# Crossbar-transposed halves joined behind the next chunk's taking apart, and kept in the slots of the later splits

## The chip, the cores and the metric

One core of one Trainium2 chip runs the whole program. The metric is the device time of one execution in microseconds; before the change it is 1086.96 us (median of 3 runs, 1085.1 to 1087.68).

## The reference, cut to what matters

Two layers; in each a half-step SwiGLU FFN, an attention mix of two branches, and a second half-step FFN. The tokens are 256, the width 1024, the FFN's inner width 2816. All is float32.

```python
def swiglu(x, w_gate, w_up, w_down):
    return (jax.nn.silu(x @ w_gate) * (x @ w_up)) @ w_down

for l in range(DEPTH):
    x = x + 0.5 * swiglu(rms_norm(x, ffn1_norm[l]), ffn1_w_gate[l], ffn1_w_up[l], ffn1_w_down[l])
    h = rms_norm(x, mix_norm[l])
    ...
    x = x + merged @ w_out[l]
    x = x + 0.5 * swiglu(rms_norm(x, ffn2_norm[l]), ffn2_w_gate[l], ffn2_w_up[l], ffn2_w_down[l])
```

## The kernel before, in words

**Products in three parts.** Every float32 operand is split into a high part (a copy rounded to the matmul's type) and a low part (the rest), and a product is three matmuls: high by high, high by low, low by high (`three`, lines 169 to 172). `split_to` (185) makes the two parts: ScalarE writes the high one (line 186, tiles wh, hi, corner, uh, vh), VectorE subtracts for the low one (187, tiles wl, lo, ul, vl). The weights stream from HBM in tiles of 512 KB: SyncE's queue (SP) loads them into a ring of four raw slots (142 and 353), and `parts` (133) splits them into a ring of six.

**The FFN** (`ffn`, 314) is called four times, two in each layer. The inner width is cut into 11 chunks of 256. For each chunk, *gate-up* runs one projection of 24 matmuls (`project`, 277) for each of the two token tiles t = 0, 1 into a PSUM bank "g", of which there are two. `glu` (447) empties it: ScalarE applies Silu to the gate half (452), VectorE multiplies by the up half (453), and both write the tile hh of the chunk. So the projection after next waits for this hh's VectorE step.

The down product needs hh transposed as float32 values are, while its layout comes from a crossbar DMA that transposes 16-bit elements. So `send` (321) takes hh apart into 16-bit halves on ScalarE (323, tile z16, "z" in the views), and SP issues the crossbar transpose into zT (325). `arrive` (328), called one chunk later than the following send, joins the halves again on ScalarE (335, tile a), adds and subtracts blocks on VectorE (340, four instructions) and splits the result into hi and lo (186, 187), which stay until the down product. `PLAN` (52) says for each chunk whether it goes into the down product plainly ("S", chunks 0, 9 and 10: four blocks, no additions) or by seven products instead of eight ("F" and "G": seven blocks). For the seven, sums of weight blocks are needed as well: `differences` (356) computes u and v from two raw rows on VectorE (357), and for three of the chunks `prepare` does so ahead, in the gate-up stage (`PREP`, 53 and 54); the others do it in `sevens` (380) during the down product. `combine` (420) folds the seven banks together at the end (p, line 427).

Who goes first. TensorE's order is as written in the code. The order on ScalarE, VectorE and SP is set by a scheduler at build time, which may move an instruction past others unless a dependency forbids it. Two rules stand in the code: `issue_after(last_hi[0])` puts the join behind the last high part written so far, and `arrive` is called at the start of chunk c for the half sent at the end of chunk c − 2. In the down product `arrive` is called in the first part and once from the third chunk on (383). Each engine works through its queue in order, so what waits holds up all behind it.

z16 shares a pair of buffers ("xg") with hh and others; zT has one buffer, and u, v and a share two ("sums").

Of the kernel before, what the change touches and what calls it, by code (L numbers as in the profile page):

```python
# [11 lines left out]
F32 = mybir.dt.float32  # L12
F32R = mybir.dt.float32r
I32 = mybir.dt.int32
BF16 = mybir.dt.bfloat16
U16 = mybir.dt.uint16
AF = mybir.ActivationFunctionType
# [5 lines left out]
P = 128  # L23
D = 1024
S = 256
# [3 lines left out]
KD = D // P  # L29
FC = 256  # L30
NFC = FF // FC
# [20 lines left out]
PLAN = "SFGFGGFGGSS"  # L52
PREP = {3: 1, 5: 3, 7: 6}
PREP_FIRST = {5: 1, 7: 3, 8: 6}
NS = sum(kind != "S" for kind in PLAN)
# [3 lines left out]
def hybrid_encoder(ctx, tc, x, w_gu1, w_d1, w_in, b_gate, qk_gain, rpb, sink, t5,  # L59
                   w_bna, w_bsw, w_out, w_gu2, w_d2, c_mask, c_band, out):  # L60
    nc = tc.nc
# [3 lines left out]
    act = ctx.enter_context(tc.tile_pool(name="act", bufs=1))  # L65
# [58 lines left out]
    def linked(engine, emit):  # L124
        with ExitStack() as order:
            if engine in chain:
                order.enter_context(tc.issue_after(chain[engine].ins))
            inst = emit()
        if chain:
            chain[engine] = inst  # L130
        return inst

    def parts(r, nk=2, n=512):
        wh = ring.tile([P, 2, 512], F32R, name="wh", tag="wh", bufs=RING)
        wl = ring.tile([P, 2, 512], F32R, name="wl", tag="wl", bufs=RING)
        split_to(wh[:, :nk, :n], wl[:, :nk, :n], r)
        return wh, wl

    def load(src, nk, n):
        raw = ring.tile([P, 2, 512], F32, name="raw", tag="raw", bufs=RAW)  # L140
        r = raw[:, :nk, :n]
        nc.sync.dma_start(r, src)
        return parts(r, nk, n)

    def columns(w, l, c0, n, nk=KD):
        return [load(w[l, 2 * i * P:(2 * i + 2) * P, c0:c0 + n].rearrange("(k p) n -> p k n", p=P), 2, n)
                for i in range(nk // 2)]

    def rows(w, l, k):
        return load(w[l, k * P:(k + 1) * P, :].rearrange("p (h n) -> p h n", h=2), 2, 512)  # L150
# [4 lines left out]
    def defer(lag, key, fn):  # L155
        later.append((now[0] + lag, len(later), key, fn))
        later.sort(key=lambda e: e[0])
# [25 lines left out]
    last_hi = [None]  # L183

    def split_to(hi, lo, src):
        last_hi[0] = linked("act", lambda: nc.scalar.activation(hi, src, AF.Copy))  # L186
        linked("dve", lambda: nc.vector.tensor_tensor(lo, src, hi.bitcast(F32), ALU.subtract))  # L187
# [126 lines left out]
    def ffn(l, n, w_gu, w_d, after):  # L314
        with tc.tile_pool(name="ffn", bufs=1) as fp:
            hs = {}
            SLOT = ((1, 2), (0, 3))

            on_way = []

            def send(c, hh):
                z = act.tile([P, 2, 4 * P], U16, name="z16", tag="xg", bufs=2)
                nc.scalar.activation(z, hh.bitcast(U16).rearrange("p s (n two) -> p two (s n)", two=2), AF.Copy)  # L323
                zT = fp.tile([P, 2 * 4, P], U16, name="zT", tag="zT")
                nc.sync.dma_start_transpose(zT, z.rearrange("p two n -> p (two n)"))
                on_way.append((c, zT))

            def arrive():
                c, zT = on_way.pop(0)
                m = 4 if PLAN[c] == "S" else 7  # L330
                hi = fp.tile([P, m, P], F32R, name=f"hi{m}", tag=f"hi{m}", bufs=NS if m == 7 else NFC - NS)
                lo = fp.tile([P, m, P], F32R, name=f"lo{m}", tag=f"lo{m}", bufs=NS if m == 7 else NFC - NS)
                a = fp.tile([P, 8, P], F32, name="a", tag="sums", bufs=2)
                with tc.issue_after(last_hi[0].ins):
                    nc.scalar.activation(a[:, :4, :].bitcast(U16).rearrange("p s (n two) -> p two (s n)", two=2),  # L335
                                         zT.rearrange("p (two s) n -> p two (s n)", two=2), AF.Copy)
                if m == 7:
                    for to, x, y, op in ((4, 0, 3, ALU.add), (6, 1, 0, ALU.subtract), (5, 4, 1, ALU.subtract),
                                         (7, 2, 5, ALU.subtract)):
                        nc.vector.tensor_tensor(a[:, to, :], a[:, x, :], a[:, y, :], op)  # L340
                    split_to(hi, lo, a[:, 1:, :])
                else:
                    split_to(hi, lo, a[:, :4, :])
                hs[c] = (hi, lo)

            def get(t, k):
# [4 lines left out]
            def block_row(k, c0=0, n=2):  # L351
                r = ring.tile([P, 2, 512], F32, name="raw", tag="raw", bufs=RAW)[:, :n, :]
                nc.sync.dma_start(r, w_d[l, k * P:(k + 1) * P, :n * 512].rearrange("p (h n) -> p h n", h=n))
                return r
# [19 lines left out]
            def sevens(c):  # L374
                r0 = block_row(2 * c, n=1 if c in stored else 2)
                r1 = block_row(2 * c + 1)
                place = ("xh0", "xl0", "xh1", "xl1")[(c - PLAN[:c].count("S")) % 4]
                both = act.tile([P, 2, 512], F32R, name="corner", tag=place)
                corner = [both[:, i, :] for i in range(2)]
                split_to(*corner, r0[:, 0, :])  # L380
                low = parts(r1)
                us, vs = stored.get(c) or differences(r0, r1, lambda name, r: parts(r))
                if on_way and c >= 2:
                    arrive()
                half = lambda pair, i: [p[:, i, :] for p in pair]
                return (("1", 0, corner), ("2", 1, half(low, 0)), ("3", 6, half(low, 1)), ("5", 3, half(us, 1)),
                        ("6", 4, half(vs, 0)), ("4", 2, half(vs, 1)), ("7", 5, half(us, 0)))
# [67 lines left out]
            for c in range(NFC):  # L455
# [4 lines left out]
                elif n == 0 and c == 1:  # L460
                    pieces = second
                else:
                    pieces = columns(w_gu, l, c * 512, 512)
# [29 lines left out]
    def mix(l, n, after):  # L493
        with tc.tile_pool(name="mix", bufs=1) as mp:
# [223 lines left out]
            def gated(br, acc, t, d):  # L718
                g = gate[br][:, t, d, :]
                nc.vector.scalar_tensor_tensor(g, g, 1.0, acc, op0=ALU.add, op1=ALU.mult)  # L720

            def local(d):
                pieces = columns(w_bsw, l, d * 512, 512, 4)
                for t in range(T):
                    acc = ps_g.tile([P, 512], F32, name="g", tag="g")
                    branch(1, acc, t, pieces, range(4))
                    gated(1, acc, t, d)
# [7 lines left out]
                split_to(*(m[:, 4 * d:4 * d + 4, :] for m in mT[t]), tp)  # L735

            def grid(d):
                pieces = columns(w_bna, l, d * 512, 512, 4)
                acc = [ps_acc.tile([P, 512], F32, name="br", tag="sc", bufs=2) for _ in range(T)]
                for ks in ((0, 1, 2), (3,)):  # L740
                    for t in range(T):
                        branch(0, acc[t], t, pieces, ks)
                for t in range(T):
                    gated(0, acc[t], t, d)
                    g = gate[0][:, t, d, :]
                    nc.vector.tensor_tensor(g, g, gate[1][:, t, d, :], ALU.add)
                    defer(M_LAG, ("merge", t, d), lambda t=t: merge(t, d))

            for d in range(2):
                local(d)  # L750
                grid(d)
# [99 lines left out]
```

## Time and profile before

| | us |
|---|---|
| median of 3 runs | 1086.96 |
| the profiled execution | 1086.75 |
| its span | 1085.0 |
| TensorE busy (PE) | 1059.2 |
| VectorE busy (DVE) | 878.1 |
| ScalarE busy (ACT) | 747.8 |

Times in the views are counted from the span's start. In the rows, L186 is line 186 of the kernel before; "out<-in" are tiles without their numbers; what stands in square brackets is the idle time before an instruction and what ended it. A matmul's recorded length is longer than the distance to the next one, because matmuls are pipelined. The first layer's FFN 1 takes about the first 190 us, its FFN 2 about 366 to 545; the second layer's FFNs stand at about 549 to 727 and 902 to 1085.

### The profile page before, as it was taken

What the parts mean: (1) busy time and instruction counts of PE and PEld (TensorE: products, weight loads), DVE (VectorE), ACT (ScalarE), POOL (GpSimd) and SP (SyncE); (2) the same over time, 40 slices, a digit from 0 to 9 for tenths busy, and PEclk for the clock granted to TensorE, in tenths of its full rate; (3) what the DMA queues carried; (4) which work ended last, traced back from release to release, by engine and by line L of the source; (5) the groups of instructions that cost most, each with busy time, mean ns of one, the idle gap of its engine ahead of it and who ended that gap; (6) DMA issues with size and microseconds to landing.
All of it is one profiled execution on the core that took longest, in us unless ns stands there. A gap on an engine that the chain in (4) does not pass through costs nothing.

```text
span 1085.0 us, 14545 instructions
## 1 busy us (share of the span) xinstructions
PE 1059.2 (98%) x4949; PEld 871.0 (80%) x4949; DVE 878.1 (81%) x1337; ACT 747.8 (69%) x1070; POOL 117.2 (11%) x118
## 2 busy tenths in 40 slices
PE   9999899999999999999999999999999999999998
PEld 7887787888888888778788778778888888877886
DVE  6677889889886868878977886998898866788796
ACT  6776855788773667776567777657887646778662
POOL 1000040244420000000000000003524100000000
PEclk9999999999999999999999999999999999999999
DMA  7988865665655578886668888658666556788753
GB/s 250 253 233 238 242 185 203 190 204 166 201 177 155 169 236 247 243 233 191 203 195 217 259 238 215 197 165 246 179 172 195 181 162 192 221 262 246 212 194 98
DMA packets 145291, 224.16 MB, mean 207 GB/s; under 512 B 54032, under 2 KB 60208, under 8 KB 145216
## 3 DMA queue, kind: packets, MB, share of 16 engines
q1 hardware_dynamic: 145024, 223.14, 69.4%
q8 instruction: 39, 0.64, 0.2%
q0 software_dynamic: 192, 0.08, 0.1%
q14 instruction: 36, 0.29, 0.1%
HBM read 210.59 MB, written 1.06 MB: 195 GB/s over the span
## 4 chain that ended last, share of the span: by engine, by line
PE 48%; DMA 22%; DVE 14%; ACT 8%; issue 7%; SPq 0%; POOL 0%; ACTq 0%; DVEq 0%; POOLq 0%
PE g L170 11%; PE g L171 11%; PE g L172 11%; DMA raw<-in_w_gu 9%; DMA raw<-in_w_d 8%; DVE wl L187 6%; DMA zT<-z 5%; ACT wh L186 4%; PE acc L171 2%; PE acc L172 2%; PE acc L170 2%; DVE u L357 2%; DVE v L357 2%; ACT z L323 2%; PE po L609 1%
## 5 line engine op out<-in xcount | busy, mean ns | idle before, releaser
L187 DVE TENSOR_TENSOR wl<-raw,wh 128x1024 fp32r<-128x1024 f32 x336 | 405.7, 1218 | 77.3 <-ACT wh L186 75.0
L186 ACT ACTIVATE wh<-raw 128x1024 fp32r<-128x1024 f32 x336 | 344.3, 1042 | 96.0 <-DMA raw<-in_w_gu 43.0
L170 PE MATMUL g<-wh,xh 128*128 128x512 f32 (+1 forms) x976 | 383.5, 393 | 11.2 <-DVE hh L453 10.7
L171 PE MATMUL g<-wl,xh 128*128 128x512 f32 (+1 forms) x976 | 377.5, 387 | 0.0
L172 PE MATMUL g<-wh,xl 128*128 128x512 f32 (+1 forms) x976 | 377.5, 387 | 0.0
L170 PEld LDWEIGHTS g<-wh,xh 128*128 128x128 f32 x976 | 183.5, 188 | 51.8 <-DVE hh L453 18.5
L172 PEld LDWEIGHTS g<-wh,xl 128*128 128x128 f32 x976 | 183.4, 188 | 38.6 <-DVE xl L187 0.6
L171 PEld LDWEIGHTS g<-wl,xh 128*128 128x128 f32 x976 | 183.7, 188 | 33.4 <-DVE wl L187 0.6
L335 ACT ACTIVATE a<-zT 128x1024 uint16<-128x1024 uint16 x44 | 60.3, 1371 | 25.0 <-DMA zT<-z 24.9
L171 PE MATMUL acc<-wl,hi 128*128 128x512 f32 x180 | 70.7, 393 | 1.6 <-DVE wl L187 1.6
L170 PE MATMUL acc<-wh,hi 128*128 128x512 f32 x180 | 71.0, 394 | 0.0
L172 PE MATMUL acc<-wh,lo 128*128 128x512 f32 x180 | 70.4, 391 | 0.0
L176 POOL TENSOR_TENSOR rs_y<-ms,mhalf 128x1 f32<-128x1 f32 x12 | 7.7, 644 | 544.8 <-DVE ms L224 536.0
L453 DVE SCALAR_TENSOR_TENSOR hh<-g,rs_y,hh 128x256 f32<-128x256 f32 x88 | 42.1, 478 | 22.3 <-ACT hh L452 22.2
L357 DVE TENSOR_TENSOR u<-raw 128x512 f32<-128x512 f32 x64 | 42.2, 690 | 21.3 <-DMA raw<-in_w_d 21.3
L187 DVE TENSOR_TENSOR lo<-a,hi 128x896 fp32r<-128x896 f32 (+1 forms) x44 | 43.1, 979 | 14.2 <-ACT hi L186 14.2
L452 ACT ACTIVATE hh<-g,rs_y 128x256 f32<-128x256 f32 x88 | 40.4, 459 | 17.0 <-PE g L172 16.6
L323 ACT ACTIVATE z<-hh 128x1024 uint16<-128x1024 uint16 x44 | 46.1, 1048 | 8.5 <-DVE hh L453 8.3
L186 ACT ACTIVATE wh<-v 128x1024 fp32r<-128x1024 f32 x20 | 21.2, 1060 | 35.8 <-DVE v L357 35.7
L587 POOL TENSOR_TENSOR S<-S,sm 128x512 f32<-128x512 f32 x32 | 37.1, 1160 | 65.8 <-DVE sm L586 40.9
L171 PEld LDWEIGHTS acc<-wl,hi 128*128 128x128 f32 x180 | 34.0, 189 | 9.7 <-DVE wl L187 2.9
L340 DVE TENSOR_TENSOR a<-a 128x128 f32<-128x128 f32 x128 | 33.0, 283 | 10.3 <-ACT a L335 10.1
(186 smaller groups left out, 1513.2 us busy)
## 6 DMA issues: line engine op xcount, KB each, us to landing
raw<-in_w_gu SPq DMA_DIRECT2D x176, 512.0 KB, 4.5
raw<-in_w_d SPq DMA_DIRECT2D x100, 512.0 KB, 4.1
raw<-in_w_in SPq DMA_DIRECT2D x64, 512.0 KB, 4.5
raw<-in_w_out SPq DMA_DIRECT2D x16, 512.0 KB, 3.6
bb<-in_b_gate SPq DMA_DIRECT2D x16, 256.0 KB, 3.4
raw<-in_w_bsw SPq DMA_DIRECT2D x8, 512.0 KB, 3.8
raw<-in_w_bna SPq DMA_DIRECT2D x8, 512.0 KB, 3.6
raw<-in_w_d SPq DMA_DIRECT2D x12, 256.0 KB, 3.4
```

The source lines that it names most:

```text
L170: nc.tensor.matmul(ps, xh, wh, start=first, stop=False)
L171: nc.tensor.matmul(ps, xh, wl, start=False, stop=False)
L172: nc.tensor.matmul(ps, xl, wh, start=False, stop=last)
L186: last_hi[0] = linked("act", lambda: nc.scalar.activation(hi, src, AF.Copy))
L187: linked("dve", lambda: nc.vector.tensor_tensor(lo, src, hi.bitcast(F32), ALU.subtract))
L323: nc.scalar.activation(z, hh.bitcast(U16).rearrange("p s (n two) -> p two (s n)", two=2), AF.Copy)
L335: nc.scalar.activation(a[:, :4, :].bitcast(U16).rearrange("p s (n two) -> p two (s n)", two=2), zT.rearrange("p (two s) n -> p two (s n)", ...
L340: nc.vector.tensor_tensor(a[:, to, :], a[:, x, :], a[:, y, :], op)
L357: sub = lambda to, x, y: nc.vector.tensor_tensor(to, x, y, ALU.subtract)
L452: linked("act", lambda: nc.scalar.activation(h, gate, AF.Silu, scale=rstd[t]))
L453: linked("dve", lambda: nc.vector.scalar_tensor_tensor(h, up, rstd[t], h, op0=ALU.mult, op1=ALU.mult))
L587: nc.gpsimd.tensor_tensor(S_, S_, sm.unsqueeze(2).to_broadcast([P, T, S]), ALU.mult)
```

## The change

The join of a chunk's halves is now ordered behind the instruction that takes the *next* chunk apart (`behind(joined, apart[c + 1])`), so it comes about one chunk later. Since two chunks' halves are then kept at once, z16 and zT no longer have their own buffers: they lie in the slots that the chunk's lo and hi tiles will take ("lo7", "hi7" or "lo4", "hi4"), which are empty until the split. The plain chunks' join gets a buffer of its own (a4) instead of one of "sums". In the down product the last `arrive` comes from the sixth chunk on instead of from the third. `columns` gets its last argument in another form, which changes nothing in the program. TensorE's and GpSimd's orders and the instructions on every engine are the same; the mix stages keep their order.

```diff
@@ -142,9 +142,13 @@
         nc.sync.dma_start(r, src)
         return parts(r, nk, n)
 
...
@@ -316,31 +320,38 @@
             hs = {}
             SLOT = ((1, 2), (0, 3))
 
-            on_way = []
+            on_way, apart = [], {}
+
+            def half(c, p, shape=None, dtype=F32R):
+                m, n = (4, NFC - NS) if PLAN[c] == "S" else (7, NS)
+                return fp.tile(shape or [P, m, P], dtype, name=p if shape else f"{p}{m}", tag=f"{p[:2]}{m}", bufs=n)
 
             def send(c, hh):
-                z = act.tile([P, 2, 4 * P], U16, name="z16", tag="xg", bufs=2)
-                nc.scalar.activation(z, hh.bitcast(U16).rearrange("p s (n two) -> p two (s n)", two=2), AF.Copy)
-                zT = fp.tile([P, 2 * 4, P], U16, name="zT", tag="zT")
-                nc.sync.dma_start_transpose(zT, z.rearrange("p two n -> p (two n)"))
+                m = 8 if PLAN[c] == "S" else 14
+                z = half(c, "lo16", [P, m, P], U16)[:, :8, :].rearrange("p s n -> p (s n)")
+                apart[c] = nc.scalar.activation(z.rearrange("p (two n) -> p two n", two=2),
+                                                hh.bitcast(U16).rearrange("p s (n two) -> p two (s n)", two=2), AF.Copy)
+                zT = half(c, "hi16", [P, m, P], U16)[:, :8, :]
+                nc.sync.dma_start_transpose(zT, z)
                 on_way.append((c, zT))
 
             def arrive():
                 c, zT = on_way.pop(0)
-                m = 4 if PLAN[c] == "S" else 7
-                hi = fp.tile([P, m, P], F32R, name=f"hi{m}", tag=f"hi{m}", bufs=NS if m == 7 else NFC - NS)
-                lo = fp.tile([P, m, P], F32R, name=f"lo{m}", tag=f"lo{m}", bufs=NS if m == 7 else NFC - NS)
-                a = fp.tile([P, 8, P], F32, name="a", tag="sums", bufs=2)
-                with tc.issue_after(last_hi[0].ins):
-                    nc.scalar.activation(a[:, :4, :].bitcast(U16).rearrange("p s (n two) -> p two (s n)", two=2),
-                                         zT.rearrange("p (two s) n -> p two (s n)", two=2), AF.Copy)
-                if m == 7:
+                if PLAN[c] == "S":
+                    a = fp.tile([P, 4, P], F32, name="a4", tag="a4")
+                else:
+                    a = fp.tile([P, 8, P], F32, name="a", tag="sums", bufs=2)
+                joined = nc.scalar.activation(a[:, :4, :].bitcast(U16).rearrange("p s (n two) -> p two (s n)", two=2),
+                                              zT.rearrange("p (two s) n -> p two (s n)", two=2), AF.Copy)
+                behind(joined, apart[c + 1] if c + 1 < NFC else last_hi[0])
+                hi, lo = half(c, "hi"), half(c, "lo")
+                if PLAN[c] != "S":
                     for to, x, y, op in ((4, 0, 3, ALU.add), (6, 1, 0, ALU.subtract), (5, 4, 1, ALU.subtract),
                                          (7, 2, 5, ALU.subtract)):
                         nc.vector.tensor_tensor(a[:, to, :], a[:, x, :], a[:, y, :], op)
                     split_to(hi, lo, a[:, 1:, :])
                 else:
-                    split_to(hi, lo, a[:, :4, :])
+                    split_to(hi, lo, a)
                 hs[c] = (hi, lo)
 
             def get(t, k):
@@ -380,7 +391,7 @@
                 split_to(*corner, r0[:, 0, :])
                 low = parts(r1)
                 us, vs = stored.get(c) or differences(r0, r1, lambda name, r: parts(r))
-                if on_way and c >= 2:
+                if on_way and c >= 5:
                     arrive()
                 half = lambda pair, i: [p[:, i, :] for p in pair]
                 return (("1", 0, corner), ("2", 1, half(low, 0)), ("3", 6, half(low, 1)), ("5", 3, half(us, 1)),
```

How the scheduler's order moves is shown at three places. The first is ScalarE round the second token tile of chunk 5 in FFN 2 of layer 0 (the same in layer 1). hh_4238 is chunk 5's gated product and hh_4331 chunk 6's; z16 or lo16 is what takes apart, a_4298 or a_4296 the join, and wh_4367, wh_4373, wh_4379 are weights for the next chunk. Before:

```order
L335 ACTIVATE a_4298<-zT_4159 128x2x512
L186 ACTIVATE wh_4367<-raw_4365 128x1024
L186 ACTIVATE vh3_4209<-v_4206 128x1024
L452 ACTIVATE hh_4238<-g_4241,rs_y_3737 128x2x128
L186 ACTIVATE wh_4373<-raw_4371 128x1024
L323 ACTIVATE z16_4268<-hh_4238 128x1024
L186 ACTIVATE hi7_4296<-a_4298 128x896
L452 ACTIVATE hh_4331<-g_4306,rs_y_3652 128x256
```

and now:

```order
L190 ACTIVATE wh_4367<-raw_4365 128x1024
L463 ACTIVATE hh_4238<-g_4241,rs_y_3737 128x2x128
L190 ACTIVATE vh3_4209<-v_4206 128x1024
L190 ACTIVATE wh_4373<-raw_4371 128x1024
L332 ACTIVATE lo16_4268<-hh_4238 128x1024
L344 ACTIVATE a_4296<-hi16_4159 128x2x512
L463 ACTIVATE hh_4331<-g_4306,rs_y_3652 128x256
L190 ACTIVATE wh_4379<-raw_4377 128x1024
L190 ACTIVATE hi7_4298<-a_4296 128x896
```

The join stood ahead of the second tile's hh and now stands behind z, ahead of the first tile's hh of the next chunk; vh moved from ahead of hh to behind it. The second place is VectorE at the same point of the program; the four additions of the join are those on a. Before:

```order
L340 TENSOR_TENSOR a_4298<-a_4298 128x128 x2
L187 TENSOR_TENSOR wl_4368<-raw_4365,wh_4367 128x1024
L340 TENSOR_TENSOR a_4298<-a_4298 128x128
L187 TENSOR_TENSOR vl3_4210<-v_4206,vh3_4209 128x1024
L453 SCALAR_TENSOR_TENSOR hh_4238<-g_4241,rs_y_3737,hh_4238 128x2x128
L340 TENSOR_TENSOR a_4298<-a_4298 128x128
L187 TENSOR_TENSOR wl_4374<-raw_4371,wh_4373 128x1024
L187 TENSOR_TENSOR lo7_4297<-a_4298,hi7_4296 128x896
L453 SCALAR_TENSOR_TENSOR hh_4331<-g_4306,rs_y_3652,hh_4331 128x256
```

and now:

```order
L191 TENSOR_TENSOR wl_4368<-raw_4365,wh_4367 128x1024
L464 SCALAR_TENSOR_TENSOR hh_4238<-g_4241,rs_y_3737,hh_4238 128x2x128
L191 TENSOR_TENSOR vl3_4210<-v_4206,vh3_4209 128x1024
L191 TENSOR_TENSOR wl_4374<-raw_4371,wh_4373 128x1024
L351 TENSOR_TENSOR a_4296<-a_4296 128x128 x3
L464 SCALAR_TENSOR_TENSOR hh_4331<-g_4306,rs_y_3652,hh_4331 128x256
L351 TENSOR_TENSOR a_4296<-a_4296 128x128
L191 TENSOR_TENSOR wl_4380<-raw_4377,wh_4379 128x1024
L191 TENSOR_TENSOR lo7_4299<-a_4296,hi7_4298 128x896
```

hh_4238 stood behind three additions and vl and now follows wl_4368 directly; three additions now stand ahead of the next chunk's hh_4331. The third place is VectorE near the end of the same FFN, where p1 and p16 fold the seven banks together and wl_5167 is the last of the down product's weights. Before:

```order
L187 TENSOR_TENSOR wl_5161<-raw_5158,wh_5160 128x1024
L427 SCALAR_TENSOR_TENSOR x0_80<-g_4812,x0_80 128x512
L427 SCALAR_TENSOR_TENSOR p1_5137<-g_4826,p1_5137 128x512
L187 TENSOR_TENSOR wl_5167<-raw_5164,wh_5166 128x1024
L427 SCALAR_TENSOR_TENSOR p16_5138<-tp_4833,p1_5137 128x512
```

and now:

```order
L191 TENSOR_TENSOR wl_5161<-raw_5158,wh_5160 128x1024
L438 SCALAR_TENSOR_TENSOR x0_80<-g_4812,x0_80 128x512
L191 TENSOR_TENSOR wl_5167<-raw_5164,wh_5166 128x1024
L438 SCALAR_TENSOR_TENSOR p1_5137<-g_4826,p1_5137 128x512
L191 TENSOR_TENSOR wl_5276<-raw_5273,wh_5275 128x1024
```

The weights' low part moved ahead of p1; it is the same in both FFNs of layer 1, and in FFN 1 of layer 0 the order stays here. On SP the crossbar transposes of chunks 2, 4 and 6 now stand ahead of two weight loads that preceded them, those of chunks 8 and 9 ahead of one, and that of chunk 10 behind one more; in FFN 1 of layer 0 the moves are of one or two loads too, at slightly other chunks.

More of the change, by code (lines that the diff above doesn't have):

```diff
@@ L143, in load, with behind, columns @@
         return parts(r, nk, n)
-    def columns(w, l, c0, n, nk=KD):
+    def behind(inst, other):
+        tc.add_manual_dep(inst.ins, other.ins.name,
+                          mybir.DependencyInfo(mybir.DependencyClass.NoSync, mybir.DependencyReason.DATA))
+    def columns(w, l, c0, n, ks=range(KD // 2)):
         return [load(w[l, 2 * i * P:(2 * i + 2) * P, c0:c0 + n].rearrange("(k p) n -> p k n", p=P), 2, n)
-                for i in range(nk // 2)]
+                for i in ks]
     def rows(w, l, k):
@@ L722, in local @@
             def local(d):
-                pieces = columns(w_bsw, l, d * 512, 512, 4)
+                pieces = columns(w_bsw, l, d * 512, 512, range(2))
                 for t in range(T):
@@ L737, in grid @@
             def grid(d):
-                pieces = columns(w_bna, l, d * 512, 512, 4)
+                pieces = columns(w_bna, l, d * 512, 512, range(2))
                 acc = [ps_acc.tile([P, 512], F32, name="br", tag="sc", bufs=2) for _ in range(T)]
```

## Prediction, made before the changed kernel had run

> **What bounds the kernel now.** I read the first part of the page, then what TensorE (PE) waited for, then the same for ScalarE (ACT) and VectorE (DVE), and last the timeline round single stalls.
>
> ```profile
> span 1085.0 us, 14545 instructions
> PE 1059.2 (98%) x4949; PEld 871.0 (80%) x4949; DVE 878.1 (81%) x1337; ACT 747.8 (69%) x1070; POOL 117.2 (11%) x118
> ```
>
> TensorE carries the span: it is recorded idle for 1085.0 − 1059.2 = 25.8 us, and its 4949 instructions are the same in the same order after the change. Only its stalls can be won, and only new stalls can be lost. This table of waits says what ended them (us in total, times, longest):
>
> ```profile
> PE g L170 <- DVE hh L453: 10.7, 9, 2.7
> PE g L171 <- DVE wl L187: 3.4, 4, 1.6
> PE tp L203 <- DVE x L308: 2.1, 5, 0.8
> PE acc L171 <- DVE wl L187: 1.6, 3, 0.5
> PE g L170 <- ACT wh L186: 0.9, 1, 0.9
> ```
>
> The largest is the gated product hh, which empties a PSUM bank "g" that the projection after next wants: 9 waits, all in the four FFNs' gate-up products. The wl and wh rows (5.9 us in 8 waits) lie in the down products. ScalarE waits 24.9 us for the crossbar, over two us of it at a time:
>
> ```profile
> ACT a L335 <- DMA zT<-z: 24.9, 24, 3.2
> ```
>
> That wait is not TensorE's. The question is how much of the 10.7 us goes with it.
>
> **A stall, and what the new order makes of it.** FFN 2 of layer 0, chunk 5. First TensorE, then ScalarE, then VectorE (start, length, engine, line, operation, idle before):
>
> ```profile
> 431.62 0.39 PE L172 MATMUL g<-wh,xl 128*128 128x512 f32 x1
> 431.84 0.39 PE L170 MATMUL g<-wh,xh 128*128 128x512 f32 x1
> ...
> 437.06 0.39 PE L172 MATMUL g<-wh,xl 128*128 128x512 f32 x1
> 438.59 0.50 PE L170 MATMUL g<-wh,xh 128*128 128x512 f32 x1 [1.15 <-DVE hh L453]
> ```
>
> ```profile
> 432.40 1.38 ACT L335 ACTIVATE a<-zT 128x1024 uint16<-128x1024 uint16 x1
> 434.49 1.06 ACT L186 ACTIVATE wh<-raw 128x1024 fp32r<-128x1024 f32 x1 [0.71 <-DMA raw<-in_w_gu]
> 435.45 1.04 ACT L186 ACTIVATE vh<-v 128x1024 fp32r<-128x1024 f32 x1
> 436.40 0.45 ACT L452 ACTIVATE hh<-g,rs_y 128x256 f32<-128x256 f32 x1
> 438.33 1.06 ACT L186 ACTIVATE wh<-raw 128x1024 fp32r<-128x1024 f32 x1 [1.47 <-DMA raw<-in_w_gu]
> 439.29 1.04 ACT L323 ACTIVATE z<-hh 128x1024 uint16<-128x1024 uint16 x1
> ```
>
> ```profile
> 435.58 1.23 DVE L187 TENSOR_TENSOR wl<-raw,wh 128x1024 fp32r<-128x1024 f32 x1 [1.06 <-ACT wh L186]
> 436.72 0.28 DVE L340 TENSOR_TENSOR a<-a 128x128 f32<-128x128 f32 x1
> 436.92 1.22 DVE L187 TENSOR_TENSOR vl<-v,vh 128x1024 fp32r<-128x1024 f32 x1
> 438.06 0.48 DVE L453 SCALAR_TENSOR_TENSOR hh<-g,rs_y,hh 128x256 f32<-128x256 f32 x1
> ```
>
> Matmuls start 0.22 to 0.23 us apart and are recorded 0.39 long, so a projection of 24 takes about 5.45 us, and each stall hides another 0.16 us in the record: 9 of them make the row's 10.7 into 12.1 us. The projection whose bank is awaited ended at 431.84; its hh ran on ScalarE at 436.40 and on VectorE at 438.06, behind the join, vh, an addition of the join and vl. In the new order (the change's ScalarE and VectorE pieces above) hh stands directly behind wh and wl. With the raw tile landing as recorded: wh 434.49 to 435.55, hh on ScalarE to 436.0; wl 435.58 to 436.81, hh on VectorE to 437.29. TensorE wants it at 437.06 + 0.23 = 437.29. The stall of 1.15 is gone or a tenth.
>
> Eight of the nine waits follow this pattern: the second token tile's hh in a chunk where v is split. The ninth, the longest, is in FFN 1 of layer 0 and awaits a first tile's hh (ScalarE, VectorE, TensorE):
>
> ```profile
> 104.39 1.06 ACT L323 ACTIVATE z<-hh 128x1024 uint16<-128x1024 uint16 x1 [1.53 <-DVE hh L453]
> 106.83 1.06 ACT L186 ACTIVATE wh<-raw 128x1024 fp32r<-128x1024 f32 x1 [1.38 <-DMA raw<-in_w_gu]
> ...
> 110.53 0.45 ACT L452 ACTIVATE hh<-g,rs_y 128x256 f32<-128x256 f32 x1
> ```
>
> ```profile
> 105.65 1.29 DVE L357 TENSOR_TENSOR u<-raw 128x512 f32<-128x512 f32 x2 [1.29 <-DMA raw<-in_w_d]
> ...
> 107.92 1.23 DVE L187 TENSOR_TENSOR wl<-raw,wh 128x1024 fp32r<-128x1024 f32 x1 [0.78 <-ACT wh L186]
> ...
> 112.34 0.47 DVE L453 SCALAR_TENSOR_TENSOR hh<-g,rs_y,hh 128x256 f32<-128x256 f32 x1
> ```
>
> ```profile
> 109.76 0.39 PE L172 MATMUL g<-wh,xl 128*128 128x512 f32 x1
> 112.87 0.50 PE L170 MATMUL g<-wh,xh 128*128 128x512 f32 x1 [2.72 <-DVE hh L453]
> ```
>
> There the new program puts z, the join, one wh and then hh on ScalarE: the join (1.38) fits into the wait for the raw tile between 105.45 and 106.83, wh ends at 107.89, hh at 108.34. On VectorE u, two additions, wl (to 109.15), one addition (0.28) and hh end at 109.91; wanted at 109.99.
>
> **What the change adds, part by part.** The instructions are the same in number and shape on every engine (the join is still one ACT of 1.38), so nothing is added to busy time. Moved work:
>
> The join now stands between z and the first tile's hh of the next chunk, with three of its four additions (0.28 each). In chunk 5, with raw landings as recorded: hh done 437.29, vh to 437.1, wh 438.33 to 439.39, z to 440.4, join to 441.8, hh on ScalarE to 442.2; the additions to 442.6, hh on VectorE to 443.1. Its bank is wanted when the second projection of chunk 6 ends, 437.29 + 5.45 = 442.7. So 0.4 us may be left here, none if that raw tile lands 0.4 earlier. I take 0.2 at each of the eight places and 0.8 us for the ninth: 2.4 us left of 12.1. **Gate-up: −9.7 us.** Bounds: −12.1 if nothing is left; an upper end comes from the rivals.
>
> u's subtractions move behind the second tile's hh, about one projection (5.45 us) later, so the raw slot of the first of its two rows is freed later, and two weight loads that stood ahead of the crossbar transpose in SP's queue in chunks 2, 4 and 6 now stand behind it. The transposes themselves come earlier, since z directly follows hh; behind each wait only raw loads. I price this at nothing: four raw slots, and wh of the next chunk is split most of a chunk (10.9 us) ahead. If that cover is gone, see the second rival.
>
> The wait for the crossbar: the joined half was sent a whole chunk earlier. The list of DMA issues gives the median from issue to landing:
>
> ```profile
> zT<-z SPq DMA_TRANSPOSE x44, 3.7
> ```
>
> 3.7 us against 10.9: the 24.9 us of ScalarE idle time go. What is late next is the raw weight tile, as in the rows above.
>
> The separate slots (z and zT in the hi and lo slots, the plain product in its own buffer) take away waits for a buffer and add none that I find: the split frees its slot before it takes it.
>
> Tail of the down product, second FFN of layer 0 and both of layer 1: in the new VectorE order a wl stands ahead of p (third piece above). VectorE first, then TensorE:
>
> ```profile
> 719.19 0.68 DVE L427 SCALAR_TENSOR_TENSOR p<-g,p 128x512 f32<-128x512 f32 x1
> 719.79 1.21 DVE L187 TENSOR_TENSOR wl<-raw,wh 128x1024 fp32r<-128x1024 f32 x1
> ```
>
> ```profile
> 721.06 0.50 PE L171 MATMUL acc<-wl,hi 128*128 128x512 f32 x1 [0.54 <-DVE wl L187]
> ```
>
> wl starts 0.60 earlier, the stall of 0.54 + 0.16 leaves 0.1, three times: **−1.8 us.**
>
> The middle of the down product: the last join moves from the third chunk to the sixth or seventh, where VectorE is full:
>
> ```profile
> 513.00:545.00 32.00, 29.73 (x130) 23.44 (x128) 29.57 (x37) 16.17 (x20) 0.00 (x0) 1.00 0.61 199
> ```
>
> VectorE is busy 29.57 of 32 us there (third number). Against that the early part loses waits like this one, 3.21 us at which ScalarE stood with VectorE behind it:
>
> ```profile
> 674.45 1.38 ACT L335 ACTIVATE a<-zT 128x1024 uint16<-128x1024 uint16 x1 [3.21 <-DMA zT<-z]
> ```
>
> The five other wl and wh waits (5.9 − 1.6 = 4.3, with 0.16 each 5.1 us) I leave as they are, **0 us**, with bounds −5.1 and +5 (as much again).
>
> One of these has a tail of its own. Windows: length, busy of PE, PEld, DVE, ACT, POOL, granted clock, DMA share, GB/s:
>
> ```profile
> 162.00:166.00 4.00, 1.46 (x6) 0.66 (x4) 3.19 (x5) 3.85 (x5) 0.00 (x0) 1.00 0.44 154
> 166.00:170.00 4.00, 4.00 (x11) 3.15 (x12) 4.00 (x5) 1.09 (x2) 0.00 (x0) 0.57 0.65 244
> 110.00:113.00 3.00, 0.28 (x2) 0.14 (x2) 3.00 (x5) 2.04 (x3) 0.00 (x0) 1.00 0.69 192
> ```
>
> After 2.54 us idle out of 4 the clock was 0.57 for the next 4 us, which costs (1 − 0.57) × 4 = 1.7 us; after one stall of 2.72 it stayed 1.00. I leave these 1.7 in place, since the stall that brings them hangs on a late raw tile, not on the join.
> The Trainium skill (TensorE: Matmul & The Clock Gate, Part 1) says that the clock halves only after an idle window of about 3.4 us. By that rule any shortening of this double stall would keep the clock up, and the sum would be 1.7 us lower.
>
> **Sum.** The profiled execution took 1086.75 us (span 1085.0 and 1.75 around it), 0.2 under the median of the runs, 1086.96. 1086.75 − 9.7 − 1.8 = 1075.25, say **1075.2 us.**
>
> **Rivals.**
> 1. *Given back in the down product.* VectorE is nearly full there, so TensorE, 9.7 us earlier in all, would only wait that much longer for the wl's. For it: 29.57 of 32. Against it: at the end of gate-up ScalarE and VectorE wait for the crossbar, the raw rows and TensorE itself, so they come earlier with it. If all of the 9.7 comes back: 1086.75 − 1.8 = 1085.0.
> 2. *Slower: raw slots.* The first row of each prepared chunk keeps one of four raw slots 5.45 us longer; the weight tile behind it lands late, ScalarE, which takes its work in order, waits for it, and both hh's behind it are late. Place: the 12 chunks of the four gate-ups in which a prepared chunk's u has just been read. For it: ScalarE already waits 0.71 and 1.47 for raw tiles in the rows above. Against it: the slots are freed by the wl's on VectorE, and those come no later than before once the join is out of their way. It decides from about 1 us of extra lateness at each place (12 × 1 is the gain). If half the 5.45, 2.7 us, arrives as lateness and 1 us of it is covered by ScalarE's freed time: 12 × 1.7 = 20.4, so 1075.2 + 20.4 = 1095.6.
> 3. *Better.* VectorE, rid of the crossbar's waits at the start of the down product, also catches up in its middle: −5.1 and the clock's −1.7 as well: 1068.4.
>
> That the join does not move is excluded: in the new order it follows the next chunk's z in every case but the last chunk's, where no later z exists.
>
> **Chances.** Forecast 0.56, rival 1 0.15, rival 2 0.12, rival 3 0.17. Two runs of this kernel can be told apart from about 0.3% on (3.3 us): faster means below 1083.7. Forecast and rival 3 lie there, and of rival 1 a quarter (0.04) for a part that stays: faster 0.77. The rest of rival 1 is the same 0.11, rival 2 is slower 0.12. Range: down to rival 3, 1068, and up to 1086 so that rival 1 is in; rival 2 and what lies below 1068 stay out.
>
> **What would show it.** Right: the waits "ACT a <- DMA zT<-z" gone or under 2 us; "PE g <- DVE hh" from 10.7 to about 2; the "PE acc <- wl" row gone; the remaining stalls in the down product. Wrong: "ACT wh <- DMA raw<-in_w_gu" well above its old sum with hh stalls at first tiles (rival 2), or the "PE g <- wl" row grown by 7 us (rival 1).

## The result, and the profile after

The changed kernel takes 1067.84 us (median of 4 runs, 1065.35 to 1069.5) against 1086.99 for the kernel before beside it (1085.1 to 1087.68). The ratio is 0.9825 (95% interval 0.9802 to 0.9847). Two more sets of runs gave 1070.86 (ratio 0.9829) and 1067.48 (0.9817). So it is faster, as forecast, but by 19 us instead of 11.5, and 0.2 us below the low end of the range.

The profiled execution of the first set is its shortest, 1065.35 us. The first part of its page:

```profile
span 1063.6 us, 14462 instructions
PE 1051.7 (99%) x4949; PEld 870.7 (82%) x4949; DVE 879.6 (83%) x1337; ACT 746.6 (70%) x1070; POOL 117.7 (11%) x118
```

What TensorE waited for in it (us in total, times, longest), and VectorE's wait for the join:

```profile
...
PE acc L175 <- DVE wl L191: 0.9, 1, 0.9
PE g L175 <- DVE wl L191: 0.4, 1, 0.4
PE g L174 <- DVE hh L464: 0.3, 2, 0.2
```

```profile
DVE a L351 <- ACT a L344: 28.1, 28, 1.2
```

The hh row went from 10.7 us in 9 waits to 0.3 in 2, and the wl rows from 5.0 in 7 to 1.3 in 2. ScalarE's wait for the crossbar is gone from its list. VectorE now waits for the join itself, 28.1 us where it was 10.1, and TensorE's hh and wl rows have not grown by it.

The stall worked through in the prediction (FFN 2 of layer 0, chunk 5) in the new trace, ScalarE, VectorE, TensorE:

```profile
426.89 1.06 ACT L190 ACTIVATE wh<-raw 128x1024 fp32r<-128x1024 f32 x1 [0.73 <-DMA raw<-in_w_gu]
427.86 0.46 ACT L463 ACTIVATE hh<-g,rs_y 128x256 f32<-128x256 f32 x1
...
430.40 1.04 ACT L332 ACTIVATE lo<-hh 128x1024 uint16<-128x1024 uint16 x1
431.34 1.35 ACT L344 ACTIVATE a<-hi 128x1024 uint16<-128x1024 uint16 x1
```

```profile
427.99 1.23 DVE L191 TENSOR_TENSOR wl<-raw,wh 128x1024 fp32r<-128x1024 f32 x1
429.13 0.48 DVE L464 SCALAR_TENSOR_TENSOR hh<-g,rs_y,hh 128x256 f32<-128x256 f32 x1
```

```profile
429.66 0.40 PE L176 MATMUL g<-wh,xl 128*128 128x512 f32 x1
429.89 0.40 PE L174 MATMUL g<-wh,xh 128*128 128x512 f32 x1
```

hh stands directly behind wh and wl and is done at 429.61. The matmul that had stalled is the second one here: it starts at 429.89, without a gap. The taking apart (lo<-hh) and the join (a<-hi) follow behind it, as drawn from the order.

**Where the time came from.** All kernels here issue the same 4949 matmuls in the same order. So the start of the n-th matmul in the trace of before, less its start in another trace, is what was gained up to there, and its growth over a stage is what that stage gave. "Down, middle" is the down product up to its last chunks, "tails" the rest of it and the first matmuls that follow. Gains in us over the profiled execution of before, four FFNs together:

| trace | gate-up | down, middle | tails | elsewhere | sum |
|---|---|---|---|---|---|
| forecast | 9.7 | 0 | 1.8 | 0 | 11.5 |
| changed, first set | 12.2 | 8.0 | 1.6 | −0.8 | 21.0 |
| changed, second set | 7.2 | 6.9 | 1.7 | −0.3 | 15.5 |
| changed, third set | 10.1 | 7.5 | 0.4 | −0.7 | 17.3 |
| mean of the three | 9.8 | 7.5 | 1.2 | −0.6 | 17.9 |

Each row is one execution. Where the tails begin and end is a choice of a few matmuls, which moves a single entry by 1 us or somewhat more and the sum not at all. From 1086.75 the mean gives 1068.9. The gate-up term stands, the tails are within 0.6, and the middle of the down product, set at 0, gave 7.5. A stall in the middle, in the kernel before (FFN 2 of layer 0):

```profile
518.44 0.50 PE L171 MATMUL g<-wl,hi 128*128 128x512 f32 x1 [0.77 <-DVE wl L187]
```

So this is the question: what cleared the middle, and the clock loss behind its worst stall, which is in the first FFN? In the profile after, TensorE runs there without a gap (us, PE busy, PEld, DVE, ACT, POOL, clock, DMA share, GB/s):

```profile
152.00:156.00 4.00, 4.00 (x20) 3.30 (x19) 4.00 (x6) 1.31 (x2) 0.00 (x0) 1.00 0.60 227
156.00:160.00 4.00, 4.00 (x19) 3.34 (x18) 3.96 (x6) 4.00 (x5) 0.00 (x0) 1.00 0.71 219
160.00:164.00 4.00, 4.00 (x19) 3.30 (x19) 4.00 (x6) 3.37 (x5) 0.00 (x0) 1.00 0.72 211
```

VectorE is full there too (11.96 of 12 us), so its load, which the prediction held against a gain here, does not by itself make TensorE stall.

### The profile page after: what moved, and what is told of

Read it like the earlier page. It is cut to its first block, busy times and chain, and to the rows that moved or that the text cites. A ratio compares the mean times of both kernels' runs of the same rounds, so it can differ in the third digit from the quotient of the medians.

```text
span 1063.6 us, 14462 instructions
## 1 busy us (share of the span) xinstructions
PE 1051.7 (99%) x4949; PEld 870.7 (82%) x4949; DVE 879.6 (83%) x1337; ACT 746.6 (70%) x1070; POOL 117.7 (11%) x118
## 4 chain that ended last, share of the span: by engine, by line
PE 55%; DVE 16%; DMA 16%; ACT 7%; issue 4%; SPq 0%; ACTq 0%; DVEq 0%
PE g L174 12%; PE g L176 12%; PE g L175 12%; DMA raw<-in_w_gu 10%; DVE wl L191 8%; DMA raw<-in_w_d 4%; PE acc L174 3%; PE acc L176 3%; PE acc L175 3%; ACT a L344 3%; ACT wh L190 2%; ACT lo L332 2%; DVE v L368 2%; PE sc L585 1%; PE po L620 1%
## 5 line engine op out<-in xcount | busy, mean ns | idle before, releaser
L190 ACT ACTIVATE wh<-raw 128x1024 fp32r<-128x1024 f32 x336 | 345.2, 1042 | 99.8 <-DMA raw<-in_w_gu 44.9
L344 ACT ACTIVATE a<-hi 128x1024 uint16<-128x1024 uint16 x44 | 59.5, 1353 | 0.0
L332 ACT ACTIVATE lo<-hh 128x1024 uint16<-128x1024 uint16 x44 | 46.2, 1051 | 18.4 <-DVE hh L464 18.3
L351 DVE TENSOR_TENSOR a<-a 128x128 f32<-128x128 f32 x128 | 32.0, 287 | 28.9 <-ACT a L344 28.1
L190 ACT ACTIVATE hi<-a 128x896 fp32r<-128x896 f32 (+1 forms) x44 | 37.7, 856 | 8.6 <-DVE a L351 8.0
L190 ACT ACTIVATE corner<-raw 128x512 fp32r<-128x512 f32 x32 | 20.0, 626 | 30.8 <-DMA raw<-in_w_d 27.6
```

Of the source, the lines that this page charges most:

```text
L332: apart[c] = nc.scalar.activation(z.rearrange("p (two n) -> p two n", two=2), hh.bitcast(U16).rearrange("p s (n two) -> p two (s n)", two= ...
L344: joined = nc.scalar.activation(a[:, :4, :].bitcast(U16).rearrange("p s (n two) -> p two (s n)", two=2), zT.rearrange("p (two s) n -> p tw ...
```

## The experiments

The change has three parts that can be told apart: the order (the join behind the next taking-apart), the buffers (z and zT in the lo and hi slots, a buffer a4 for the plain chunks' join), and the place of the last join (c >= 5 instead of c >= 2). Theory A: the late last join cleared the middle. Rival B: the order did. Rival C: the buffers did.

**Changed kernel, early last join.**

```diff
-                if on_way and c >= 5:
+                if on_way and c >= 2:
```

> The changed kernel with the last chunk's join back at the down product's third chunk (c >= 2). By index of the matmul, the changed kernel gained some 11.8 us in the four gate-ups, 6.3 us in stalls in the middle of the down products, 1.6 us of clock behind one of them, and 1.5 us net at the tails. Theory A (the late last join brought the middle): 6.3 + 1.6 = 7.9 us come back, 1067.8 + 7.9 = 1075.7, with stalls on wl in the middle of the down products as before the change. Rival B (the join's place behind the next taking-apart brought the middle too, because the early part of the down product no longer waits for the crossbar): 1068, no such stalls. Rival C (the slots brought it): 1068 as well.

1069.88 us, ratio 0.9857 (0.9831 to 0.9883). Gains: gate-up 14.3, middle 6.5, tails 1.2. Theory A's 1075.7 is out.

**Kernel before, late last join.**

```diff
-                if on_way and c >= 2:
+                if on_way and c >= 5:
```

> The kernel before with only the last join moved to the sixth or seventh chunk (c >= 5). Theory A: the middle's 7.9 us go, the gate-up's 12.1 stay: 1087.0 - 7.9 = 1079. Rival B: 1087 within 1, the middle's stalls stand. Rival C: 1087. In every case PE g <- DVE hh stays near 10.7 us.

1088.11 us, ratio 1.0006 (0.9984 to 1.0029): nothing. But the trace is no copy of before: the middle gave 7.6 and the tails lost 3.2. (The profiled execution took 1082.89 us, 5.2 under the median of its runs, so its sum is not a gain of the runs.) The stalls on wl in the middles are gone, and at the tails of the three later FFNs they are longer (1.33, 1.20, 0.69 against 0.54 each):

```profile
533.77 0.50 PE L171 MATMUL acc<-wl,hi 128*128 128x512 f32 x1 [1.33 <-DVE wl L187]
715.84 0.50 PE L171 MATMUL acc<-wl,hi 128*128 128x512 f32 x1 [1.20 <-DVE wl L187]
1067.82 0.50 PE L171 MATMUL acc<-wl,hi 128*128 128x512 f32 x1 [0.69 <-DVE wl L187]
```

In the old buffers the stall of the later FFNs goes where the last join goes. That speaks against rival B too: the middle was cleared here in the old order.

**Buffers alone.** The changed kernel with

```diff
-                if on_way and c >= 5:
+                if on_way and c >= 2:
...
-                joined = nc.scalar.activation(a[:, :4, :].bitcast(U16).rearrange("p s (n two) -> p two (s n)", two=2),
-                                              zT.rearrange("p (two s) n -> p two (s n)", two=2), AF.Copy)
-                behind(joined, apart[c + 1] if c + 1 < NFC else last_hi[0])
+                with tc.issue_after(last_hi[0].ins):
+                    nc.scalar.activation(a[:, :4, :].bitcast(U16).rearrange("p s (n two) -> p two (s n)", two=2),
+                                         zT.rearrange("p (two s) n -> p two (s n)", two=2), AF.Copy)
```

> The changed kernel's buffers (both crossbar halves in the split's slots, a buffer of its own for the plain join), but the old order (join after the last split that was issued) and the early last join. Theory A and rival B: nothing moves, 1087 within 1.5, ACT a <- DMA near 25 us and PE g <- DVE hh near 10.7. Rival C: transposes that no longer wait for a buffer bring the middle's 7.9, 1079.

1078.09 us, ratio 0.9928 (0.9902 to 0.9953). This is rival C's 1079. Gate-up −2.3, middle 8.0, tails 3.7. In TensorE's waits hh stands first and no wl at all:

```profile
PE g L174 <- DVE hh L464: 13.4, 15, 2.2
...
```

**Order alone.** The kernel before with

```diff
-                with tc.issue_after(last_hi[0].ins):
-                    nc.scalar.activation(a[:, :4, :].bitcast(U16).rearrange("p s (n two) -> p two (s n)", two=2),
-                                         zT.rearrange("p (two s) n -> p two (s n)", two=2), AF.Copy)
+                joined = nc.scalar.activation(a[:, :4, :].bitcast(U16).rearrange("p s (n two) -> p two (s n)", two=2),
+                                              zT.rearrange("p (two s) n -> p two (s n)", two=2), AF.Copy)
+                behind(joined, apart[c + 1] if c + 1 < NFC else last_hi[0])
```

> The kernel before with only the join's place changed (behind the next chunk's taking-apart); old buffers, early last join. The transpose of a chunk must now wait until the join before it has read the one zT. Theory A: the gate-up's 11.8 and the tails' 1.5 go, the middle's stalls stay: 1087.0 - 13.3 = 1073.7. Rival B: 1067 to 1068. Rival C (a transpose held up by the single zT holds up the raw loads behind it in SP's queue): above 1080, with ACT wh <- DMA raw well above its 43 us.

1078.99 us, ratio 0.9938 (0.9916 to 0.996): above theory A's 1073.7, below rival C's 1080. Gate-up 10.7, middle −4.8, tails −0.1. (The profiled execution is the longest of its runs, 1082.09, so the −4.8 may be on the high side.) The hh row falls to 1.3, the wl rows grow:

```profile
PE g L175 <- DVE wl L191: 6.0, 9, 0.9
...
PE acc L175 <- DVE wl L191: 1.7, 3, 0.6
...
PE g L174 <- DVE hh L457: 1.3, 4, 0.4
```

So far: the order carries the gate-up and only that; the buffers carry the middle. The next runs ask which buffer. Theory D: a4. The plain chunks' join took one of the two slots "sums" that the down product's u and v also take; with a4 it takes none. Rival E: z and zT in slots of their own.

**Own buffer a4 and zT in the hi slot, old order.** (zT keeps its new place, so no run here has a4 without it.) As in the run of the buffers alone, but

```diff
-                z = half(c, "lo16", [P, m, P], U16)[:, :8, :].rearrange("p s n -> p (s n)")
+                z = act.tile([P, 8 * P], U16, name="z16", tag="xg", bufs=2)
```

> The kernel before with two of the three buffer changes: a buffer of its own for the plain chunks' join, and zT in the split's hi slot (without that the own buffer does not fit); z stays where it was, the old order and the early last join stay. With all three buffer changes the middle of the down products gave 8.0 us and the tails 3.7, 1078.1. Theory D (the plain join's own buffer brings it: it no longer shares two slots with u, v and the prepared joins): 1078 within 2, no stall on wl in the middle. Rival E (z and zT in their own slots bring it): 1083 to 1087, the middle's stalls there.

1078.14 us, ratio 0.9907 (0.9889 to 0.9925). Gate-up −2.4, middle 8.0, tails 5.2, as theory D has it.

**z and zT in the slots, no a4, old order.** As in the run of the buffers alone, but

```diff
-                if PLAN[c] == "S":
-                    a = fp.tile([P, 4, P], F32, name="a4", tag="a4")
-                else:
-                    a = fp.tile([P, 8, P], F32, name="a", tag="sums", bufs=2)
+                a = fp.tile([P, 8, P], F32, name="a", tag="sums", bufs=2)
...
```

> The kernel before with the other pair: z and zT in the split's slots, the plain join still in the shared buffer. Theory D: 1087 within 2, the middle's stalls of before. Rival E: 1078 within 2, none.

1092.18 us, ratio 1.0042 (1.0025 to 1.0059): slower than before, which neither theory had. Gate-up −4.6, middle 1.2, tails −1.4. The middle's stalls stand (0.77 each in FFN 2 of layer 0 and FFN 1 of layer 1, where before has 0.77 and 0.76), so rival E is out. The loss lies in the gate-up:

```profile
PE g L174 <- DVE hh L461: 16.2, 15, 3.2
PE g L175 <- DVE wl L191: 4.5, 7, 0.8
```

**Changed kernel without a4.** The same edit on the changed kernel (new order, late last join).

> The changed kernel, with the new order, the late last join and both half slots, but with the plain join in the shared buffer as before. Theory D: the middle's 6.3 and the clock's 1.6 come back at least in part, and more as in the run with the order alone, 1073 to 1079. Rival E: 1068 within 1.5.

1076.55 us, ratio 0.9897 (0.9879 to 0.9915). Gate-up 11.0, middle 1.0, tails −2.5. This too is as theory D has it, and the stall is again at the place of the last join, now the later one (FFN 2 of layer 0: 529.69, where the run with the order alone has it at 515.98):

```profile
529.69 0.50 PE L175 MATMUL g<-wl,hi 128*128 128x512 f32 x1 [0.63 <-DVE wl L191]
```

**The changed kernel again, and three neighbours of it.**

> The changed kernel once more, on the chip of these runs and with more rounds. 1068 within 1.5, ratio 0.982 to 0.986. If the late last join is worth something beside slots and order, this is under the ratio of the run with the early last join (0.9857, 0.9831 to 0.9883) by more than 0.003; if not, the two intervals lie over one another. Stalls: hh under 1 us in all, none on wl in the middle, and the one of 1 us at the tail of the first down product should be there again if it belongs to the order and not to that execution.

1070.86 us, ratio 0.9829 (0.9805 to 0.9852). The hh row was under 1 us in the first profile and is not here, and one stall on wl, 0.59 us, stands in the middle of the first down product, so those parts of the expectation were wrong; the stall at the first down product's tail is there again (1.3):

```profile
PE g L174 <- DVE hh L464: 4.3, 8, 1.3
...
PE g L175 <- DVE wl L191: 1.4, 3, 0.6
PE acc L175 <- DVE wl L191: 1.3, 1, 1.3
```

> The changed kernel for the two before it: 1066 to 1071, ratio 0.981 to 0.987.

1067.48 us, ratio 0.9817 (0.9793 to 0.9842).

Beside it, in the same set of runs, the early last join once more:

> The changed kernel with the early last join, beside the changed kernel in the same call. The late place was worth 7.9 us in theory A, which the first such run contradicts (ratio 0.9857). With the plain join's own buffer the place should be worth nothing: within 2 us of the changed kernel of this call, either sign.

1070.64 us, ratio 0.9832 (0.9808 to 0.9855): 3.2 us above the changed kernel of this set, where within 2 was expected. The intervals lie over one another, so with a4 the place of the last join is worth nothing that these runs can tell.

And the changed kernel with z back in the shared act slots (the edit of the own-buffer run):

> The changed kernel with z back in the shared act slots (zT in the hi slot, the plain join in its own buffer, new order, late last join). If, as theory D says, only the plain join's own buffer and the order carry the change: as the changed kernel, within 2 us of it, no stall on wl in the middle. If z's slot matters (a z that waits in the shared slots holds up hh): 4 us or more above it, with more hh stalls.

1067.44 us, ratio 0.9818 (0.9785 to 0.985): as the changed kernel. z's own slot is worth nothing that these runs can tell. One part of the expectation was missed: a stall on wl of 1.07 us stands in the middle of the first down product.

**The clock by itself.** The changed kernel whole, and behind its last result bursts of matmuls with stalls ahead of them:

```diff
...
+    def stall(k):
+        for _ in range(k):
+            nc.vector.tensor_copy(gap[:, 0, :128], xs[1][:, 896:])
+    def dense(n):
+        for _ in range(n):
+            nc.tensor.matmul(bank, gap[:, 0, :P], gap[:, 0, :], start=True, stop=True)
...
+    for k in (2, 4, 6, 8, 10, 12, 14, 16, 20):
+        for n in (60, 65, 71):
+            stall(k)
+            dense(n)
+    for k in (2, 3, 4, 5, 6, 7):
+        for n in (60, 65, 71):
+            stall(k)
+            dense(1)
+            stall(k)
+            dense(n)
```

> The changed kernel and, behind its last result, some 45 bursts of 60 to 71 dense matmuls with one stall of 2 to 20 small VectorE copies ahead of each, or two stalls split by one matmul. It measures the clock's price by itself. If the clock follows one unbroken idle window of about 3.4 us (the Trainium skill, TensorE: Matmul & The Clock Gate, Part 1), stalls under that cost nothing but themselves, split or not. If it follows the share of idle time in a window that runs on by itself, as the run with the order alone (1.39 and 0.76 idle, then 0.50) and the kernel before (one stall of 2.72, then 1.00) suggest, then from some 2 us of idle on some bursts start at half clock and others of the same stall do not, and split stalls act like whole ones.

Start, length, matmuls and the stall ahead. A burst at full clock takes 13.9 (60), 15.0 (65) and 16.4 us (71), and does so behind every single stall of up to 1.63 us. Three stalls of 2.15, three of 3.7, and a pair of 1.10 split by one matmul:

```profile
1223.16 13.91 PE L794 MATMUL g<-gap 128*128 128x512 f32 x60 [2.15 <-DVE gap L790]
1239.23 16.65 PE L794 MATMUL g<-gap 128*128 128x512 f32 x65 [2.15 <-DVE gap L790]
1258.02 16.41 PE L794 MATMUL g<-gap 128*128 128x512 f32 x71 [2.15 <-DVE gap L790]
```

```profile
1393.96 16.79 PE L794 MATMUL g<-gap 128*128 128x512 f32 x60 [3.71 <-DVE gap L790]
1414.47 17.88 PE L794 MATMUL g<-gap 128*128 128x512 f32 x65 [3.72 <-DVE gap L790]
1436.06 16.39 PE L794 MATMUL g<-gap 128*128 128x512 f32 x71 [3.72 <-DVE gap L790]
```

```profile
1687.44 0.50 PE L794 MATMUL g<-gap 128*128 128x512 f32 x1 [1.10 <-DVE gap L790]
1689.05 15.53 PE L794 MATMUL g<-gap 128*128 128x512 f32 x60 [1.10 <-DVE gap L790]
...
```

Of three stalls of 2.15 one costs 1.6 us more (16.65 for 15.03), of three of 3.7 two cost 2.9, the third nothing. Between them, one of three stalls of 2.67 and all three of 3.2 cost time. Each of the three pairs of 1.10 costs 1.6 like a whole stall of 2.15; pairs of 0.84 cost nothing. So the price does not follow one unbroken stall; the last section shows what it follows.

## Why the prediction was wrong in size

**Gate-up, −9.7: right.** The three traces of the changed kernel give 12.2, 7.2 and 10.1, mean 9.8, and the order alone 10.7. The forecast left 2.4 us of stalls; the runs show 0.3 to 4.3 in the hh row. With such a spread, a mean that meets the term to 0.1 is partly luck. That the spread comes from when raw tiles land is likely but was not followed.

**Tail of the down product, −1.8: about right, but it is a4's.** The three stalls of 0.54 went, with wl ahead of p. The order of the join does not bring that: in the run with the order alone p still stands ahead of wl and the stalls are 0.54, 0.57 and 0.57, while in both runs with a4 and the old order wl stands ahead and they are gone. Not forecast: a stall of 0.9 to 1.3 at the tail of the first down product, where wl stands behind x and p on VectorE:

```profile
175.66 0.68 DVE L438 SCALAR_TENSOR_TENSOR x<-g,x 128x512 f32<-128x512 f32 x1
176.26 0.68 DVE L438 SCALAR_TENSOR_TENSOR p<-g,p 128x512 f32<-128x512 f32 x1
176.86 1.21 DVE L191 TENSOR_TENSOR wl<-raw,wh 128x1024 fp32r<-128x1024 f32 x1
```

**The failed step: the middle of the down product "as they are, 0 us", with the buffers said to "take away waits for a buffer and add none that I find" and then given no price.** The middle and its clock loss gave 6.9 to 8.0 us. The prediction looked for what the buffers remove among the recorded waits and named only ScalarE's wait for the crossbar. The shared slot has no row of its own there: it shows as order. In the kernel before, the first v of the down product takes the slot that the plain chunk's join holds, so it stands behind that join's last reader, lo. VectorE, FFN 2 of layer 0, before:

```profile
488.71 1.30 DVE L357 TENSOR_TENSOR u<-raw 128x512 f32<-128x512 f32 x2 [1.79 <-DMA raw<-in_w_d]
...
493.11 0.68 DVE L187 TENSOR_TENSOR lo<-a,hi 128x512 fp32r<-128x512 f32 x1
...
495.45 0.69 DVE L357 TENSOR_TENSOR v<-raw,u 128x512 f32<-128x512 f32 x1
```

The same with the buffers alone, and with z and zT moved but the slot still shared:

```profile
484.21 0.69 DVE L368 TENSOR_TENSOR u<-raw 128x512 f32<-128x512 f32 x1 [1.80 <-DMA raw<-in_w_d]
484.82 0.68 DVE L368 TENSOR_TENSOR v<-raw,u 128x512 f32<-128x512 f32 x1
```

```profile
491.55 1.29 DVE L365 TENSOR_TENSOR u<-raw 128x512 f32<-128x512 f32 x2 [1.38 <-DMA raw<-in_w_d]
...
500.25 0.69 DVE L191 TENSOR_TENSOR lo<-a,hi 128x512 fp32r<-128x512 f32 x1 [0.78 <-ACT hi L190]
500.98 0.69 DVE L365 TENSOR_TENSOR v<-raw,u 128x512 f32<-128x512 f32 x1
```

With a4, v follows u directly. With the shared slot it comes 6.7 and 9.4 us after u started, behind lo. TensorE is 3.9 us ahead in the run of the buffers alone at that place, v 10.6 us. v is the last reader of a raw row, and SP's next load waits for that row, so the late tiles ("corner", "wl") behind the stalls of before are the far end of this chain. The last steps of the chain do stand in the record: a later v is what ScalarE waits for here, its wl ends at 518.38 on VectorE, and the stall of 0.77 shown further up ends at 518.44.

```profile
516.06 1.06 ACT L186 ACTIVATE wh<-v 128x1024 fp32r<-128x1024 f32 x1 [1.42 <-DVE v L357]
```

ScalarE's row for that wait, before and after (before, it is longer than the crossbar's 24.9 us, and the prediction passed over it):

```profile
ACT wh L186 <- DVE v L357: 35.7, 17, 4.1
```

```profile
ACT wh L190 <- DVE v L368: 10.0, 8, 2.4
```

It is a pointer, not a measure: it is 25 to 48 us in the five traces with the shared slot and 9 to 29 in the eight with a4 (the run with the bursts left aside). The prediction itself quotes the head of such a chain, a join that waits 3.21 us for the crossbar, and reads only ScalarE's time from it, not the slot that it keeps from v.

Shown by runs: with the shared slot the middle stalls, or the stall moves with the last join (order alone, z and zT moved, late join alone, changed without a4). With a4, in either order and at either place, no stall on wl is left in the middles of the three later FFNs; in the first FFN four of the eight traces have such stalls, 1.07 us at most. Argued, not shown apart: that the slot acts through v and the raw rows, and not through other rows of the order that move with it; a third slot "sums" instead of a4 was not tried, nor a4 with zT in its old buffer.

**Clock, 1.7 "left in place, since the stall that brings them hangs on a late raw tile, not on the join": wrong.** With a4 the double stall of the first down product (0.92 and 1.62) is gone and the clock stays 1.00 there. The join's slot is one cause of the late raw tile by the argument above, but not the only thing that clears this place: with z and zT moved and the slot shared the two stalls are 0.38 and 0.76, with the late join alone there are none, and in both the clock stayed 1.00. So what part of this loss belongs to a4 is open.

**The rivals.** The third ("better") came true in its number, 1068.4, and not in its way: the order alone rids ScalarE of the crossbar's waits, and the middle lost 4.8 there; what cleared it was a slot. That the number fits is luck. The first (all given back) is refuted by the middle's gain, though with the order alone 4.8 of 10.7 us were given back there in the one trace: without a4 it would have been half right. The second (raw slots, slower) did not happen: "ACT wh <- DMA raw<-in_w_gu" is 44.9 us against 43.0. The late last join, from which the prediction drew the middle's bounds, is worth nothing measurable once a4 is there.

Order and buffers about add up: 8.2 and 9.1 us alone by the medians, 16 to 21 together. Open: why the moved buffers lose 2.3 to 4.6 us in the gate-up under the old order, and what of the tails' 3.7 to 5.2 with a4 and the old order the new order gives back.

## What to carry to other kernels

A buffer that two unrelated steps share by tag is a dependency between them; price it by finding, for each taker of the slot, the last reader of the one before, since in a scheduled program it can appear as an instruction's place and not as a wait. When stalls remain that "hang on a late load", follow the load back to the instruction that freed its slot before calling them independent of the change. The start of the n-th matmul in two traces, subtracted, shows by stage where a change paid and where it was given back, which the totals of a wait table don't.

## What the runs showed of the hardware

The clock's loss does not follow the length of one stall alone: in the last run one stall of 2.15 us in three cost clock, one of 3.72 cost nothing, and two of 1.10 with a matmul between them cost 1.6 us. The traces show what it follows. In every run the granted clock changes only at edges of one grid of 3.413 us that runs on by itself (in the last run 48 changes, none more than 2 ns off the grid), and what decides is how long TensorE is recorded idle within one window of that grid. Windows of the last run, laid on its grid (us, PE busy, PEld, DVE, ACT, POOL, clock, DMA share, GB/s):

```profile
1219.22:1222.63 3.41, 1.79 (x8) 1.14 (x7) 1.37 (x7) 0.00 (x0) 0.00 (x0) 1.00 0.00 0
1222.63:1226.04 3.41, 2.88 (x13) 2.37 (x14) 0.44 (x2) 0.00 (x0) 0.00 (x0) 1.00 0.01 2
...
1236.29:1239.70 3.41, 1.26 (x6) 0.76 (x5) 1.82 (x8) 0.00 (x0) 0.00 (x0) 1.00 0.00 0
1239.70:1243.12 3.42, 3.42 (x10) 2.65 (x9) 0.00 (x0) 0.00 (x0) 0.00 (x0) 0.50 0.00 0
...
1430.85:1434.26 3.41, 1.50 (x7) 0.92 (x5) 1.64 (x8) 0.00 (x0) 0.00 (x0) 1.00 0.00 0
1434.26:1437.67 3.41, 1.61 (x7) 1.35 (x8) 1.54 (x7) 0.00 (x0) 0.00 (x0) 1.00 0.02 5
1437.67:1441.09 3.42, 3.42 (x17) 2.83 (x16) 0.00 (x0) 0.00 (x0) 0.00 (x0) 1.00 0.00 0
```

The first stall of 2.15 lies across an edge, 1.62 us idle in one window and 0.53 in the next, and costs nothing. The second lies within one window, and the next window runs at half clock. The stall of 3.72 that cost nothing is cut into 1.91 and 1.80. Over all fourteen traces, a window at full clock with up to 1.69 us of recorded idle time was always followed by full clock, and one with more than 1.91 always by half clock; of the 13 between, 7 were followed by half. That is about half a window. The kernels show the same: the stall of 2.72 that left the clock at 1.00 in the kernel before lies across an edge, 1.38 and 1.34, and with the order alone the stalls of 1.39 and 0.76 lie in one window, and the next one has 0.50.

The Trainium skill (TensorE: Matmul & The Clock Gate, Part 1) has a free-running window of some 3.4 us and says that the clock halves after an idle one. The window agrees with these traces, in length too; but it need not be idle throughout, since some 1.9 us of its 3.4 were enough.

The second unexpected thing is the spread: the changed kernel's runs go from 1065.35 to 1071.91 us, and its hh row from 0.3 to 4.3, with the same instructions in the same order.
